# Key-innermost factors for the weight-table products of a two-layer PEER transformer kernel

## The chip, the cores and the metric

One core of one Trainium2 chip. The metric is the device time of one execution in microseconds. Three executions of the kernel before took 4184.06, 4193.06 and 4194.59 us; the median is 4193.06 us.

## The reference, cut to what matters

The reference is a transformer of two layers over 512 latent tokens and 256 context tokens, width 1024. Each layer is modulated by a conditioning vector (`silu(c) @ ada_w + ada_b`, six blocks of 1024 columns), has an attention (global in layer 0, windowed in layer 1), and ends in a PEER mixer: each token picks, in each of 8 heads, 16 of 128 x 128 experts, and mixes them with gates.

```python
def peer_block(hb, w_q, sub_keys, u_tab, v_tab):
    ...
    v1, i1 = lax.top_k(s1, PEER_TOPK)
    v2, i2 = lax.top_k(s2, PEER_TOPK)
    ...
    top_s, pos = lax.top_k(cand_s, PEER_TOPK)
    expert = jnp.take_along_axis(cand_i, pos, axis=-1)   # i1 * 128 + i2
    g = jax.nn.softmax(top_s, axis=-1)
    u = u_tab[expert]
    act = jax.nn.gelu(jnp.einsum('nhkd,nd->nhk', u, hb).astype(jnp.float32))
    w = (g * act).astype(hb.dtype)
    return jnp.einsum('nhk,nhkd->nd', w, v_tab[expert])
```

The output is the latent stream after both layers.

## The kernel before, in words

**Dense and sparse tokens.** Most tokens' PEER is computed densely, over all 16384 experts: a table G holds, for each token, the gate of each expert (zero where it isn't picked), and the dense part multiplies the gelu of `h @ u` by G before it multiplies by `v`. In layer 0 all 512 latent tokens (4 tiles of 128) are dense and the 256 context tokens are gathered one by one; in layer 1 the last 384 latent tokens (3 tiles) are dense and the first 128 are gathered.

**build_g** (L524) makes G for a tile of 128 tokens. Its input is a PSUM bank that `topk_resolve` (L478) leaves: for each of a token's 128 picks (8 heads x 16) the first key, the second key and the gate, with the pick on the partition axis. For a token, G is a product over the picks: one factor is the one-hot of the second key (128 picks x 128 keys), the other the one-hot of the first key times the gate, so 128 products of 128x128x128 for each tile. A step takes TB = 8 tokens: VectorE compares keys with a counter (`hot`, L547: both one-hots, bf16, laid out [pick, 2, key, token], token innermost), VectorE multiplies the first by the gate (`Eg`, L550, f32, [pick, key, token]), ScalarE casts the second to f32 (`B`, L552), and TensorE makes 8 products (`gm`, L557), four into a PSUM bank. A matmul reads its operands as `B[:, :, k]` and `Eg[:, :, k]`, so with a step of 8 floats from key to key. Each f32 product shows in the trace as two matmuls and two weight loads, 16 of each in a step. Banks are emptied one behind (LAG = 1) by ScalarE (L537): it reads the bank in its own order (token, then key) and writes `gsb` [key, 32 tokens] with the 32 tokens innermost, so 32 floats apart from key to key. After 4 steps (32 tokens) a `gsb` (2 buffers) is stored to the DRAM table Gd by SP's queue (L154, 2 MB).

**Buffers.** `hot` uses the tag "wh" and `B` the tag "wl", two buffers each, in the weight pool wp (layer 0) or gp (layer 1); `Eg` has two in gp. `topk_resolve` has one buffer each of the tags "hot" and "rep" in the pool kt: for each of its two key tables it writes `rep` (a copy by ScalarE, L511), `hot` (a comparison by VectorE, L513), multiplies them (L514) and sums on TensorE (L516).

**Conditioning.** `ada_load` (L180) issues 16 loads of 512 KB of `ada_w` on SP's queue, and `ada_cols` (L191) multiplies them with the conditioning vectors (`pr`, L198), transposes and adds the bias. Group 1 of layer 0 is loaded after the projections of its attention; groups 0 to 2 of layer 1 are loaded and multiplied after the build_g of the first three tiles of layer 0. All of these use the tag "wr" in the pool wp, WR = 4 buffers. `load_split` (L156) uses the same pool for projection weights: raw in "wr", its high and low halves in "wh" and "wl" (2 buffers each).

**Order of the work.** The kernel is written with a tile framework: each engine's instructions, and SP's queue of transfers, run in order, with semaphores set from the tiles that they touch. After build_g the dense part starts: it loads G back as `Gt` (L657), multiplies with `u` (`sp`) and `v` (`kp`, `op`), while gathers for the sparse tokens run on GpSimd. Some of its first weights (`Ur`, L154 to L162) are loaded and split during build_g.

Of the kernel before, what the change touches and what calls it, by code (L numbers as in the profile page):

```python
# [10 lines left out]
F32 = mybir.dt.float32  # L11
F32R = mybir.dt.float32r
BF16 = mybir.dt.bfloat16
U32 = mybir.dt.uint32
AF = mybir.ActivationFunctionType
ALU = mybir.AluOpType
# [4 lines left out]
P = 128  # L21
# [13 lines left out]
NK = 128  # L35
CB = 128
CBA = 512
# [5 lines left out]
TB = 8  # L43
# [16 lines left out]
WR = 4  # L60
# [9 lines left out]
def body(ctx, tc, xT_in, cT_in, ada_w, ada_b, gains1, gains2, w_qkv, qk_gain, w_o, sinks,  # L70
         w_pq, subk, u_t, u_n, v_b, v_n, ropeC, ropeS, ropeR, out):
    nc = tc.nc
    V, A, G, T = nc.vector, nc.scalar, nc.gpsimd, nc.tensor
# [7 lines left out]
    def bank(tag, name, bufs):  # L81
        return ps.tile([P, 512], F32, tag=tag, name=name, bufs=bufs)
# [9 lines left out]
    o = 0  # L92
# [10 lines left out]
    iota_t = const.tile([P, NK, TB], BF16, name="iota_t")  # L103
# [45 lines left out]
    def nm(s):  # L149
        uid[0] += 1  # L150
        return f"{s}_{uid[0]}"

    def dma(dst, src):
        nc.sync.dma_start(dst, src)  # L154
# [22 lines left out]
        modT = res.tile([P, 48, 2], F32, tag=f"mod{L}", name=nm("mod"))  # L177
        return modT

    def ada_load(L, grp, pool, bufs, between=None, tag="ar"):  # L180

        raws = []
        for i in range(16):
            if between:
                between(i)
            raw = pool.tile([P, 2, CBA], F32, tag=tag, name=nm(tag), bufs=bufs)
            dma(raw, ada_w[L, grp * 4 + i % 4, :, 2 * (i // 4):2 * (i // 4) + 2])
            raws.append(raw)
        return raws

    def ada_cols(L, modT, grp, pool, raws):  # L191


        pr = bank("S", nm("pr"), 2)
        for kt in range(DT):
            for j in range(4):
                js = slice(32 * j, 32 * j + 32)
                T.matmul(pr[js], cst[:, kt], raws[kt // 2 * 4 + j][:, kt % 2], start=kt == 0, stop=kt == DT - 1,  # L198
                         skip_group_check=True)
        rows = pool.tile([P, CBA], F32, tag="rows", name=nm("rows"), bufs=1)  # L200
        A.copy(rows, pr)
        pc = bank("bg", nm("pc"), 4)
        for i in range(4):
            T.transpose(pc[:, i * P:(i + 1) * P], rows[:, i * P:(i + 1) * P], ident)
        got = pc.rearrange("p (i j c) -> p j i c", j=4, c=32)[:, :, :, 0:2]
        blk = slice(grp * 16, grp * 16 + 16)
        bias = adb[:, L, blk].rearrange("p (j i) -> p j i", i=4)[:, :, :, None].to_broadcast([P, 4, 4, 2])
        V.tensor_tensor(modT[:, blk, :].rearrange("p (j i) c -> p j i c", i=4), got, bias, ALU.add)
# [312 lines left out]
    def flat(a):  # L521
        return a.rearrange("p h k -> p (h k)")

    def build_g(pt, Gd, t, gp, pe):  # L524


        ib = gp.tile([P, 2, P], BF16, tag="ib", name=nm("ib"), bufs=2)
        A.copy(ib.rearrange("p a b -> p (a b)"), pt[:, :2 * P])
        gt = gp.tile([P, P], F32, tag="gt", name=nm("gt"), bufs=2)
        A.copy(gt, pt[:, 2 * P:3 * P])  # L530
        full = [P, NK, TB]
        HT = TB // 2
        pending = []

        def evacuate():
            po, gs, o, b = pending.pop(0)
            A.copy(gs[:, :, o:o + HT].rearrange("p a t -> p t a"), po.rearrange("p (t a) -> p t a", t=HT))  # L537
            if o + HT == GB:
                dma(Gd[:, :, t * (P // GB) + b].rearrange("s p f -> p s f"),
                    gs.rearrange("p (s a) t -> p s (a t)", a=SC))  # L540

        for b in range(P // GB):
            gs = gp.tile([P, NK, GB], F32, tag="gsb", name=nm("gsb"), bufs=GSB)
            for n8 in range(GB // TB):
                tok = slice(b * GB + n8 * TB, b * GB + (n8 + 1) * TB)
                hot = pe.tile([P, 2] + full[1:], BF16, tag="wh", name=nm("hot"), bufs=2)
                V.tensor_tensor(hot, iota_t[:, None].to_broadcast([P, 2] + full[1:]),  # L547
                                ib[:, :, None, tok].to_broadcast([P, 2] + full[1:]), ALU.is_equal)
                Eg = gp.tile(full, F32, tag="Eg", name=nm("Eg"), bufs=2)
                V.tensor_tensor(Eg, hot[:, 0], gt[:, None, tok].to_broadcast(full), ALU.mult)  # L550
                B = pe.tile(full, F32, tag="wl", name=nm("B"), bufs=2)
                A.copy(B, hot[:, 1])  # L552
                for half in range(2):
                    po = bank("bg", nm("gm"), 4)
                    for i in range(HT):
                        k = half * HT + i
                        T.matmul(po[:, i * P:(i + 1) * P], B[:, :, k], Eg[:, :, k], start=True, stop=True)  # L557
                    pending.append((po, gs, (n8 * 2 + half) * HT, b))
                    if len(pending) > LAG:
                        evacuate()  # L560
        while pending:
            evacuate()
# [164 lines left out]
    mods = [ada_begin(L) for L in range(DEPTH)]  # L727
# [3 lines left out]
    for L in range(DEPTH):  # L731
        last = L == DEPTH - 1
        modT = mods[L]
        b1, g1, b2, g2 = (modT[:, i * DT:(i + 1) * DT, :] for i in (0, 2, 3, 5))
        stiles = list(range(SPARSE[L]))
        c0 = SPARSE[L] * P if last else 0
        nd = NLAT - c0
        groups = (LAT,) if last else (LAT, CTX)
        Gd = dram.tile([NK // SC, P, nd // GB, SC * GB], F32, tag=f"G{L}", name=nm("Gd"))
# [9 lines left out]
        if last:  # L749
            kt = kt_es.enter_context(pool(f"kt{L}"))  # L750
        wp = wp_es.enter_context(pool(f"wp{L}"))
        with pool(f"sp{L}") as sp, ExitStack() as a0_es:
            if L == 0:
                a0 = a0_es.enter_context(pool("a0"))
                def between(i):
                    if i in (4, 8):
                        half = slice(i - 4, i)
                        dma(xl[:, half], xT_in[:, half, :NLAT])
# [10 lines left out]
        with pool(f"ap{L}") as ap:  # L769
            r = qkv(L, wp, ap)  # L770
            if L == 0:
                ada_cols(0, modT, 1, wp, ada_load(0, 1, wp, WR, tag="wr"))
            if not last:
                attention(CTX, L, blocks_ctx, *r, ap, False)
                attention(LAT, L, blocks_global, *r, ap, False)
            else:
                attention(LAT, L, blocks_window, *r, ap, True)
# [16 lines left out]
        if not last:  # L794
            kt = kt_es.enter_context(pool(f"kt{L}"))
# [19 lines left out]
        with pool(f"gp{L}") as gp:  # L815
            for t in range(c0 // P, NLAT // P):
                topk_scan(tk["l", t], v12["l", t], 1, kt)
                pt = topk_resolve(tk["l", t], i12["l", t], kt, "bg", lambda i, shape: kt.tile(
                    shape, BF16, tag=("hot", "rep")[i], name=nm("hot"), bufs=1))
                build_g(pt, Gd, t - c0 // P, gp, gp if last else wp)  # L820
                if not last:
                    if t < 3:
                        ada_cols(1, mods[1], t, wp, ada_load(1, t, wp, WR, tag="wr"))
        if not last:
            kt_es.close()
            wp_es.close()
# [1 line left out]
        with pool(f"db{L}") as db:  # L828
            rb = rb_es.enter_context(pool(f"rb{L}", right=True))
            sg = groups[-1]["nm"]  # L830
            with pool(f"kc{L}") as kc:
                prep = []
                for t in stiles:
                    with later(SLACK2):
                        for hb in range(2):
                            topk_scan(tk[sg, t], v12[sg, t], hb, kc)
                        pt = topk_resolve(tk[sg, t], i12[sg, t], kc, "O", lambda i, shape: rb.tile(
                            shape, BF16, tag=("gu", "gv")[i], name=nm("hot"), bufs=(GUB, GVB)[i]))
# [90 lines left out]
```

## Time and profile before

| | us |
|---|---|
| median of 3 executions | 4193.06 |
| lowest, highest | 4184.06, 4194.59 |
| the profiled execution | 4188.21 |
| its span, first to last instruction | 4186.4 |
| TensorE matmul busy | 3962.7 (95%) |
| VectorE busy | 2979.7 (71%) |
| ScalarE busy | 1552.6 (37%) |
| GpSimd busy | 997.7 (24%) |
| mean granted clock of TensorE | 0.980 |

The profile names engines PE (TensorE matmuls), PEld (TensorE weight loads), DVE (VectorE), ACT (ScalarE), POOL (GpSimd) and SP (the transfers' queue). A group of instructions shows its line, engine, operation, output and inputs, shapes and count, then busy time and the mean of one in ns, then how long the engine sat idle before it and what ended that. A busy TensorE is not one at its peak: matmuls overlap, so the distance between two starts says more than the duration of one.

### The profile page before, as it was taken

The page shows a single profiled execution, that of the slowest core. Times are in us where ns is not written, and L with a number is a line of the kernel's source. Part 1 is how long each engine was busy: PE and PEld are TensorE (multiplying, and loading weights), DVE is VectorE, ACT ScalarE, POOL GpSimd, SP SyncE. Part 2 cuts the span into 40 slices and gives each one's busy share as a digit, 9 for nine tenths or more (in the row PEclk, how much of TensorE's full clock was granted, in tenths as well). Part 3 has the DMA queues.
Part 4 walks back from the last instruction along what each step waited for, and adds up shares of the span by engine and source line. Part 5 has one row for each costly group of instructions (what it writes and reads, how often), then busy time and mean ns, then how long its engine had stood idle before and what let it go on. Part 6 is the DMA issues. An engine that isn't in the chain of part 4 may idle for free.

```text
span 4186.4 us, 52018 instructions
## 1 busy us (share of the span) xinstructions
PE 3962.7 (95%) x19384; PEld 3405.7 (81%) x19384; DVE 2979.7 (71%) x5857; ACT 1552.6 (37%) x2271; POOL 997.7 (24%) x778
## 2 busy tenths in 40 slices
PE   7999898898899999999999989999998999999999
PEld 5667677687788777777777767768997999999999
DVE  3273796546688888888888754669657778787875
ACT  3162326556222222222222233534773333333332
POOL 0000000000344545444544300000002344443420
PEclk9999999999999999999999999999999999999999
DMA  4203125545699899989898831121457888888874
GB/s 175 97 20 112 56 79 167 166 136 175 209 323 329 315 316 322 327 315 316 316 330 310 285 107 60 32 74 36 131 144 260 286 292 299 302 300 297 299 270 157
DMA packets 343406, 894.08 MB, mean 214 GB/s; under 512 B 25968, under 2 KB 145904, under 8 KB 338800
## 3 DMA queue, kind: packets, MB, share of 16 engines
q1 hardware_dynamic: 232560, 488.05, 34.2%
q0 software_dynamic: 110592, 402.70, 28.1%
q8 instruction: 152, 2.49, 0.2%
q14 instruction: 102, 0.84, 0.1%
HBM read 826.16 MB, written 64.49 MB: 213 GB/s over the span
## 4 chain that ended last, share of the span: by engine, by line
PE 57%; issue 16%; DMA 11%; POOL 7%; DVE 7%; ACT 2%; SPq 0%; POOLq 0%; DVEq 0%; ACTq 0%
PE gm L557 10%; DMA gv<-v_n,idx 6%; PE sp L168 5%; PE sp L170 5%; PE sp L169 5%; PE pj L168 4%; PE pj L169 4%; PE pj L170 4%; POOL gu L593 4%; POOL gv L593 3%; DMA gu<-u_n,idx 3%; PE kp L676 2%; PE kp L678 2%; PE kp L677 2%; PE op L678 2%
## 5 line engine op out<-in xcount | busy, mean ns | idle before, releaser
L593 POOL DMA_INDIRECT gu<-u_n,idx x384 | 544.6, 1418 | 2816.2 <-DVE idx L573 1070.1
L168 PE MATMUL sp<-hil,Uh 128*128 128x512 f32 (+1 forms) x2048 | 751.5, 367 | 27.1 <-ACT act L654 27.1
L169 PE MATMUL sp<-lol,Uh 128*128 128x512 f32 (+1 forms) x2048 | 752.0, 367 | 0.0
L170 PE MATMUL sp<-hil,Ul 128*128 128x512 f32 (+1 forms) x2048 | 746.7, 365 | 4.2 <-DVE Ul L162 4.2
L621 DVE SCALAR_TENSOR_TENSOR acc<-gv,w,acc 128x1024 f32<-128x1024 f32 x381 | 490.0, 1286 | 134.7 <-DMA gv<-v_n,idx 133.9
L662 ACT CAST wh<-act 128x512 fp32r<-128x512 f32 (+1 forms) x256 | 145.0, 567 | 1034.2 <-DVE act L660 1026.2
L593 POOL DMA_INDIRECT gv<-v_n,idx x384 | 450.0, 1172 | 327.6 <-DVE acc L621 220.6
L611 DVE CUSTOM_DVE_ANT_0 gu<-gu,hn 128x1024 f32<-128x1024 f32 x384 | 468.5, 1220 | 69.1 <-DMA gu<-u_n,idx 68.4
L557 PEld LDWEIGHTS gm<-Eg,B 128*128 128x128 f32 x1792 | 432.4, 337 | 25.9 <-issue 11.4
L557 PE MATMUL gm<-Eg,B 128*128 128x128 f32 x1792 | 439.7, 422 | 11.1 <-DVE Eg L550 10.8
L168 PEld LDWEIGHTS sp<-hil,Uh 128*128 128x128 f32 x2048 | 387.3, 189 | 75.7 <-ACT act L654 28.1
L162 DVE TENSOR_TENSOR Ul<-Ur,Uh 128x1024 fp32r<-128x1024 f32 x256 | 312.5, 1221 | 190.7 <-ACT Uh L160 190.6
L170 PEld LDWEIGHTS sp<-hil,Ul 128*128 128x128 f32 x2048 | 387.2, 189 | 50.8 <-DVE Ul L162 6.1
L677 PE MATMUL kp<-wh,Vl 128*128 128x512 f32 (+1 forms) x1024 | 378.5, 370 | 49.8 <-DVE Vl L162 49.8
L169 PEld LDWEIGHTS sp<-lol,Uh 128*128 128x128 f32 x2048 | 387.8, 189 | 40.6 <-issue 2.5
L160 ACT CAST Uh<-Ur 128x1024 fp32r<-128x1024 f32 x256 | 268.9, 1051 | 395.3 <-PE sp L169 389.7
L676 PE MATMUL kp<-wh,Vh 128*128 128x512 f32 (+1 forms) x1024 | 376.3, 368 | 1.7 <-ACT wh L662 1.3
L678 PE MATMUL kp<-wl,Vh 128*128 128x512 f32 (+1 forms) x1024 | 376.1, 367 | 0.0
L676 PE MATMUL op<-wh,Vh 128*128 128x512 f32 (+1 forms) x1024 | 371.4, 363 | 0.3 <-DVE xl L647 0.3
L677 PE MATMUL op<-wh,Vl 128*128 128x512 f32 (+1 forms) x1024 | 370.5, 362 | 0.0
L678 PE MATMUL op<-wl,Vh 128*128 128x512 f32 (+1 forms) x1024 | 370.5, 362 | 0.0
L160 ACT CAST Vh<-Vr 128x1024 fp32r<-128x1024 f32 x256 | 268.8, 1050 | 222.5 <-PE op L678 186.1
(223 smaller groups left out, 6554.9 us busy)
## 6 DMA issues: line engine op xcount, KB each, us to landing
Ur<-u_t SPq DMA_DIRECT2D x256, 512.0 KB, 5.9
Vr<-v_b SPq DMA_DIRECT2D x256, 512.0 KB, 6.6
Gd<-gsb SPq DMA_DIRECT2D x28, 2048.0 KB, 9.3
wr<-ada_w SPq DMA_DIRECT2D x64, 512.0 KB, 5.4
Gt<-Gd SPq DMA_DIRECT2D x32, 1024.0 KB, 8.1
Gt<-Gd SPq DMA_DIRECT2D x32, 768.0 KB, 7.1
ar<-ada_w SPq DMA_DIRECT2D x32, 512.0 KB, 10.2
wr<-w_pq SPq DMA_DIRECT2D x32, 512.0 KB, 3.6
```

The costliest lines, as they stand in the source:

```text
L160: A.copy(hi, raw)
L162: V.tensor_tensor(lo, raw, hi, ALU.subtract)
L168: T.matmul(o, sh, mh, start=i == 0, stop=False)
L169: T.matmul(o, sh, ml, start=False, stop=False)
L170: T.matmul(o, sl, mh, start=False, stop=i == n - 1)
L557: T.matmul(po[:, i * P:(i + 1) * P], B[:, :, k], Eg[:, :, k], start=True, stop=True)
L593: G.indirect_dma_start(out=r, out_offset=None, in_=tab, in_offset=bass.IndirectOffsetOnAxis(ap=idx[:, s:s + 1], axis=0))
L611: V.tensor_tensor_reduce(out=r, in0=r, in1=hn, scale=1.0, scalar=0.0, op0=ALU.mult, op1=ALU.add, accum_out=sd[:, k:k + 1])
L621: V.scalar_tensor_tensor(acc[ti], r, w[:, k:k + 1], acc[ti], ALU.mult, ALU.add)
L676: T.matmul(o[:, :n], vh[:, k, ds], wh, start=start, stop=False, skip_group_check=True)
L677: T.matmul(o[:, :n], vl[:, k, ds], wh, start=False, stop=False, skip_group_check=True)
L678: T.matmul(o[:, :n], vh[:, k, ds], wl, start=False, stop=stop, skip_group_check=True)
```

## The change

The one-hots keep their layout, token innermost, but the two f32 factors are written as [pick, token, key], so that a matmul reads `second[:, k]` and `first[:, k]` as 128 contiguous floats. The product with the gate (VectorE) and the cast (ScalarE) therefore read `hot` with a step of 8 bf16 from key to key. The bank is read with the token innermost (512 bytes apart) and `gsb` is written in groups of four contiguous floats; each fourth bank is emptied by VectorE. The one-hots of the steps alternate between the tags "hot" and "rep" of the pool kt, one buffer each, which topk_resolve uses too. "wh" and "wl" of wp are no longer used by build_g, and the conditioning loads that took 4 buffers of "wr" take 8 in turn: 4 of "wr", 2 of "wh", 2 of "wl".

```diff
-    def ada_load(L, grp, pool, bufs, between=None, tag="ar"):
+    def ada_load(L, grp, pool, bufs, between=None):
...
-            raw = pool.tile([P, 2, CBA], F32, tag=tag, name=nm(tag), bufs=bufs)
+            tag, n = ("ar", bufs) if bufs else (("wr", WR), ("wr", WR), ("wh", 2), ("wl", 2))[i // 2 % 4]
+            raw = pool.tile([P, 2, CBA], F32, tag=tag, name=nm(tag), bufs=n)
...
-    def build_g(pt, Gd, t, gp, pe):
+    def build_g(pt, Gd, t, gp, kp):
...
-            A.copy(gs[:, :, o:o + HT].rearrange("p a t -> p t a"), po.rearrange("p (t a) -> p t a", t=HT))
+            count[0] += 1
+            eng = V.tensor_copy if count[0] % 4 == 0 else A.copy
+            eng(gs[:, :, o:o + HT], po.rearrange("p (t a) -> p a t", t=HT))
...
-                hot = pe.tile([P, 2] + full[1:], BF16, tag="wh", name=nm("hot"), bufs=2)
-                V.tensor_tensor(hot, iota_t[:, None].to_broadcast([P, 2] + full[1:]),
-                                ib[:, :, None, tok].to_broadcast([P, 2] + full[1:]), ALU.is_equal)
-                Eg = gp.tile(full, F32, tag="Eg", name=nm("Eg"), bufs=2)
-                V.tensor_tensor(Eg, hot[:, 0], gt[:, None, tok].to_broadcast(full), ALU.mult)
-                B = pe.tile(full, F32, tag="wl", name=nm("B"), bufs=2)
-                A.copy(B, hot[:, 1])
+                hot = kp.tile([P, 2, NK, TB], BF16, tag=("hot", "rep")[n8 % 2], name=nm("hot"), bufs=1)
+                V.tensor_tensor(hot, iota_t[:, None].to_broadcast([P, 2, NK, TB]),
+                                ib[:, :, None, tok].to_broadcast([P, 2, NK, TB]), ALU.is_equal)
+                first = gp.tile([P, TB, NK], F32, tag="first", name=nm("first"), bufs=2)
+                V.tensor_tensor(first, hot[:, 0].rearrange("p a t -> p t a"),
+                                gt[:, tok, None].to_broadcast([P, TB, NK]), ALU.mult)
+                second = gp.tile([P, TB, NK], F32, tag="second", name=nm("second"), bufs=2)
+                A.copy(second, hot[:, 1].rearrange("p a t -> p t a"))
...
-                        T.matmul(po[:, i * P:(i + 1) * P], B[:, :, k], Eg[:, :, k], start=True, stop=True)
+                        T.matmul(po[:, i * P:(i + 1) * P], second[:, k], first[:, k], start=True, stop=True)
...
-                ada_cols(0, modT, 1, wp, ada_load(0, 1, wp, WR, tag="wr"))
+                ada_cols(0, modT, 1, wp, ada_load(0, 1, wp, 0))
...
-                build_g(pt, Gd, t - c0 // P, gp, gp if last else wp)
+                build_g(pt, Gd, t - c0 // P, gp, kt)
...
-                        ada_cols(1, mods[1], t, wp, ada_load(1, t, wp, WR, tag="wr"))
+                        ada_cols(1, mods[1], t, wp, ada_load(1, t, wp, 0))
```

## Rows read from the trace of the kernel before

**Rows 1.** The page, chain that ended last: shares by engine, then by line.
```profile
PE 57%; issue 16%; DMA 11%; POOL 7%; DVE 7%; ACT 2%; SPq 0%; POOLq 0%; DVEq 0%; ACTq 0%
PE gm L557 10%; DMA gv<-v_n,idx 6%; PE sp L168 5%; PE sp L170 5%; PE sp L169 5%; PE pj L168 4%; PE pj L169 4%; PE pj L170 4%; POOL gu L593 4%; POOL gv L593 3%; DMA gu<-u_n,idx 3%; PE kp L676 2%; PE kp L678 2%; PE kp L677 2%; PE op L678 2%
```

**Rows 2.** Line 557: its durations (min/median/max), its waits, and who waited (us, times).
```profile
L557 PEld LDWEIGHTS gm<-Eg,B x1792: 312/338/343, 643.7 to 3130.5; 128*128 128x128 f32 x200
...
  DVE Eg L550: 10.8, 4
...
who waited for it (us, times):
  DVE Eg L550: 180.3, 98
  ACT gsb L537: 143.8, 149
```

**Rows 3.** Stretches, all engines: us; PE, PEld, DVE, ACT, POOL busy; clock; DMA; GB/s.
```profile
640.00:990.00 350.00, 319.42 (x1376) 276.78 (x1375) 185.72 (x257) 209.75 (x225) 0.00 (x0) 0.97 0.51 153
...
794.00:826.00 32.00, 19.62 (x92) 8.43 (x92) 15.77 (x52) 9.48 (x13) 0.00 (x0) 0.84 0.69 222
...
2908.00:3132.00 224.00, 217.89 (x985) 216.41 (x985) 138.81 (x172) 163.94 (x179) 0.00 (x0) 0.98 0.43 122
```

**Rows 4.** The same stretches, line 557 alone: us; PE, PEld busy; clock; DMA; GB/s.
```profile
640.00:990.00 350.00, 252.68 (x1024) 247.32 (x1024) 0.97 0.51 153
2908.00:3132.00 224.00, 187.05 (x768) 185.08 (x768) 0.98 0.43 122
```

**Rows 5.** Timeline in build_g: start, us, engine, line, operation, shapes, count.
```profile
670.59 15.43 PEld L557 LDWEIGHTS gm<-Eg,B 128*128 128x128 f32 x64 [0.84 <-issue]
```

**Rows 6.** Timeline in peer_q: products of the same shape, operands contiguous.
```profile
593.04 0.97 PEld L439 LDWEIGHTS s<-skb,pq 128*128 128x128 f32 x8 [0.23 <-ACT pq L436]
```

**Rows 7.** Groups by line and form, ScalarE.
```profile
L537 ACT COPY gsb<-gm 128x512 f32<-128x512 f32 x224 | 232.0, 1036 | 145.7 <-PE gm L557 143.8
L552 ACT CAST B<-hot 128x1024 f32<-128x1024 bf16 x112 | 118.8, 1062 | 7.1 <-DVE hot L547 7.0
...
L405 ACT COPY pT<-pt 128x512 f32<-128x512 f32 x48 | 27.5, 588 | 18.2 <-PE pt L398 18.2
```

**Rows 8.** Groups by line and form, VectorE.
```profile
L550 DVE TENSOR_TENSOR Eg<-hot,gt 128x1024 f32<-128x1024 bf16 x112 | 136.6, 1225 | 180.3 <-PE gm L557 180.3
L547 DVE TENSOR_TENSOR hot<-iota_t,ib 128x2048 bf16<-128x2048 bf16 x112 | 132.0, 1219 | 3.6 <-ACT ib L528 3.4 <-ACT B L552 0.2
...
L405 DVE COPY pT<-pt 128x256 f32<-128x256 f32 x32 | 13.4, 419 | 3.3 <-PE pt L398 2.7
...
L387 DVE TENSOR_TENSOR su<-su 128x1 f32<-128x1 f32 x48 | 7.6, 158 | 12.6 <-ACT pr L383 12.6
...
L405 DVE COPY pT<-pt 128x128 f32<-128x128 f32 x16 | 4.6, 290 | 3.0 <-PE pt L398 3.0
...
L485 DVE COPY gs<-ts 128x8 f32<-128x8 f32 x10 | 1.6, 160 | 0.0
```

**Rows 9.** Timeline in build_g, VectorE: two comparisons in a row.
```profile
670.86 2.35 DVE L547 TENSOR_TENSOR hot<-iota_t,ib 128x2048 bf16<-128x2048 bf16 x2
```

**Rows 10.** Timeline at the first tile border: a copy and a comparison of topk_resolve.
```profile
719.31 1.90 ACT L511 COPY hot<-dif 128x2048 bf16<-128x2048 bf16 x1
...
785.34 1.22 DVE L513 TENSOR_TENSOR hot<-posb,first_pos 128x2048 bf16<-128x2048 bf16 x1
```

**Rows 11.** Waits from 590 to 1000 us: us in total, times, longest.
```profile
PE pr L198 <- DMA wr<-ada_w: 19.4, 8, 11.1
```

**Rows 12.** Waits from 160 to 210 us: us in total, times, longest.
```profile
PE pr L198 <- DMA wr<-ada_w: 8.5, 6, 3.1
```

**Rows 13.** The page, DMA issues: count, KB each, median us to landing.
```profile
Gd<-gsb SPq DMA_DIRECT2D x28, 2048.0 KB, 9.3
wr<-ada_w SPq DMA_DIRECT2D x64, 512.0 KB, 5.4
```

More of the change, by code (lines that the diff above doesn't have):

```diff
@@ L530, in build_g @@
         A.copy(gt, pt[:, 2 * P:3 * P])
-        full = [P, NK, TB]
         HT = TB // 2
         pending = []
+        count = [0]
         def evacuate():
             po, gs, o, b = pending.pop(0)
-            A.copy(gs[:, :, o:o + HT].rearrange("p a t -> p t a"), po.rearrange("p (t a) -> p t a", t=HT))
+            count[0] += 1
+            eng = V.tensor_copy if count[0] % 4 == 0 else A.copy
+            eng(gs[:, :, o:o + HT], po.rearrange("p (t a) -> p a t", t=HT))
             if o + HT == GB:
```

## The prediction

> **What bounds the kernel now.** The clock comes first: TensorE's granted clock is 0.97 and 0.98 in the two stretches that matter [rows 3], its upper level (2.4 GHz), so it is not the issue. The chain that ended last comes second: TensorE has 57% of it, and its largest single line is L557, the small products of build_g, with 10% [rows 1]; 10% of the 4186 us span is some 420 us. Third, who waits for whom at L557: VectorE's Eg (L550) waited 180 us for these matmuls and ScalarE's gsb copy (L537) 144 us, while the matmuls themselves sat idle 11 us for Eg and nearly nothing else [rows 2]. So in build_g TensorE sets the pace. Fourth, how long that is: build_g runs in 640 to 990 us (layer 0, 4 tiles, 64 steps of 8 tokens) and 2908 to 3132 us (layer 1, 3 tiles, 48 steps); L557 alone is busy 252.7 and 187.1 us there [rows 4].
>
> Fifth, why it is slow. Undisturbed, 64 weight loads (4 steps) take 15.43 us [rows 5], so 0.24 us for each and 3.84 us for the 16 of a step. The products of peer_q have the same shape and type (128x128x128 f32), but operands that lie contiguous: 8 weight loads take 0.97 us [rows 6]. With a load's own 0.19 us taken off the end, 7 spacings take 0.78 us: 0.111 us each. In build_g each operand B[:, :, k] and Eg[:, :, k] is read with 8 floats, 32 bytes, from one key to the next. That is the only difference that I find between the two.
>
> **The change, part by part.** *Matmuls.* The same 1792 instructions, with the operands contiguous. At 0.111 us a step takes 16 x 0.111 = 1.78 us of TensorE instead of 3.84. TensorE then no longer sets the pace, and the question is which of the other two engines does.
>
> *VectorE, per step.* The comparison (hot, L547) stays: two in a row take 2.35 us, one of them 1.22, so the second adds 1.13 [rows 8, 9]. The product with the gate, `first` (Eg before, L550, 1.225 us), has as many elements and still writes contiguously, but reads the bf16 hot 16 bytes apart. Its lower bound is 1.13 us, as now; the upper one comes from the weight load: (0.240 - 0.111)/128 = 1.01 ns more per strided element, times 1024 is 1.03 us more, so 2.16 us. I take 1.13: the row is the same instruction with as many elements, and a copy of 8 elements 64 bytes apart takes 160 ns against 158 for an operation on one [rows 8]. These rows are small and of different operations, so both ends are kept. One bank in four now goes to VectorE, half a bank per step. A copy of 256 elements from a bank takes 419 ns and of 128 takes 290: 1.01 ns per element, so 0.68 us for 512. For the stride I add what ScalarE now pays for its own: 1.036 us for the strided bank copy against 0.588 for a plain 128x512 one, 0.45 us more [rows 7, 8]. That gives 1.13 us, bounds 0.68 and 1.58 (twice the excess); half is 0.56. Sum: 1.13 + 1.13 + 0.56 = 2.82 us, bounds 2.60 and 4.08.
>
> *ScalarE, per step.* The cast `second` (B, 1.06 us) also reads 16 bytes apart: 1.06 to 2.09. One and a half bank copies remain: now they write four floats together but read the bank 512 bytes apart. I keep 1.04, the same copy with its stride on the other side; bounds 0.59 and 1.48. Sum: 1.06 + 1.5 x 1.04 = 2.62, bounds 1.95 and 4.31.
>
> So VectorE sets 2.82 us per step: (3.84 - 2.82) x 112 = **114 us less**. The 144 us of both stretches that are no steps (574 - 112 x 3.84) stay in length: TensorE's other work inside them (66.7 and 30.8 us [rows 3, 4]) now hides under VectorE, while VectorE's own other work (the scan of the next tile, the Ul splits) comes into the open. VectorE's other work is 56 us there (324.5 busy [rows 3], less 112 times the two instructions of rows 8). I put the two against each other, with 20 us either way.
>
> What the rule would make of `first`: the Trainium skill (SBUF — State Buffer, section Door 1: The DMA port swizzle) says that SBUF lines are 16 bytes, and that a stream which goes to a new line at each access pays for it. Here every read of hot by key does that, so the rule speaks for the upper end; the weight loads agree with it at 32 bytes, and no row shows it for VectorE's reads at 16. By the row that I take the sum is 4070 us, by the rule it is rival 1's, below.
>
> *hot in two single buffers shared with topk_resolve.* The steps alternate between "hot" and "rep", so as many are in flight as before. But now a tile's resolve can't start its rep copy (1.90 us, L511) before the last steps have let go of that buffer. Before, ScalarE made it a whole tile early, at 719 us, while the comparison that needs it came at 785 [rows 10]. It now stands beside that comparison (1.22 us) at each of 5 tile borders: about 2 us each, **10 us more**, bounds 0 and 20.
>
> *Conditioning loads in 8 buffers.* TensorE waits 19.4 us for them in layer 0's stage, and 8.5 us of its 28 us at 178 to 206, where attention stands behind them on TensorE [rows 11, 12]. Half of that goes, **14 us less**, bounds 0 and 28: buffers wh and wl come free only when the last projections have been multiplied. On SP's queue the loads stand in line with the Gd stores, so an earlier load also frees a store behind it. The stores themselves have as many bytes; each lands in 9.3 us [rows 13], under four new steps (11.3 us), so two gsb buffers still cover it, with only 2 us to spare.
>
> The profiled execution took 4188.2 us, 5 below the median of the runs shown. Sum: 4188 - 114 + 10 - 14 = **4070 us**. What comes after each stretch (the dense part) starts as much earlier, since its first matmuls wait for Gt, read from Gd.
>
> **The rivals.**
> 1. *VectorE reads slowly by key.* With `first` at 2.16 us the step takes 1.13 + 2.16 + 0.56 = 3.85 us, and the whole gain of the steps is gone: 4185 us; half the excess gives 4127. For it: TensorE's weight loads. Against: the two small copies above. The rule cited above gives this same outcome.
> 2. *ScalarE becomes the bound, and slower than TensorE was.* The place is its queue of cast and bank copies. It decides from the point where cast + 1.5 bank copies pass 3.84 us: with the cast at 2.09 that is a bank copy over 1.17 us. At 1.48, twice the excess, the step takes 4.31 us: 112 x 0.47 = 53 more, so 4237 us. For it: ScalarE's excess on strided writes [rows 7], and that it is now asked for two kinds of strided reads. Against: bank copies lose their strided writes, and a quarter of them.
>    The Trainium skill (PSUM — Partial Sum Buffer, section Specifications (TRN2)) gives PSUM lines of 8 bytes and says that non-contiguous patterns slow matmuls a lot; whether a copy out of a bank pays too, no row shows.
> 3. *Transfers become the bound in layer 0.* A tile writes 8 MB of G and loads 8 MB of weights for the next layer. If a store takes 16 us beside the loads instead of 11.3 for its four steps, 12 stores x 4.7 = 56 us come back: 4126 us. For it: the queues move 222 GB/s at a tile's border [rows 3]. Against: the DMA engines are 51% busy over that stretch.
> 4. *The change doesn't quicken the loads,* because the stride is not what slows them; all stays at some 4185 us. Against it: rows 6.
>
> **How the numbers follow.** The forecast has 0.47 and its own range of 4030 to 4105 (the bank copy at its lower bound takes 25 off, the small terms move the rest), rival 1 0.22, rival 2 0.13, rival 3 0.12, rival 4 0.06. I predict 4070 us. The range leaves out rival 2 and the lowest edge of the forecast: 4035 to 4195. 0.3%, some 12.6 us, is about what a measurement can tell from no change. Faster by more: the forecast, rival 3 and half of rival 1, 0.70. Within: the other half and most of rival 4, 0.16. Slower: rival 2 and a rest, 0.14.
>
> **What would show it right or wrong.** Weight loads of the small products 0.11 us apart, no longer followed by VectorE waiting for TensorE; `first` near 1.2 us and a bank copy near 1.0; VectorE without gaps through a tile, and 16 steps in some 45 us instead of 61. Wrong: `first` over 2 us (rival 1), bank copies over 1.2 with VectorE waiting on ScalarE's order (rival 2), gsb copies waiting for Gd stores (rival 3), weight loads still at 0.24 us (rival 4).

## The result, and the profile after

The changed kernel takes 4044.27 us (median of 4 runs, 4038.29 to 4048.38) against 4192.49 us before (a fourth run added to the three above): a ratio of 0.9649, 95% interval 0.9629 to 0.9669. So it is 148 us faster; 4070 us had been forecast. The profiled execution took 4048.38 us with a span of 4046.6, so 139.8 us less span than before.

The chain that ended last, on the page of the changed kernel (shares by engine, then by line):

```profile
PE 49%; issue 19%; DVE 13%; DMA 10%; POOL 8%; ACT 2%; POOLq 0%; SPq 0%; DVEq 0%; ACTq 0%
PE sp L170 5%; DMA gv<-v_n,idx 5%; PE sp L168 5%; PE sp L169 5%; DVE first L554 4%; POOL gv L598 4%; POOL gu L598 4%; PE pj L168 4%; PE pj L169 4%; PE pj L170 4%; DMA gu<-u_n,idx 3%; PE kp L682 2%; PE kp L683 2%; PE kp L681 2%; PE op L683 2%
```

The small products (now line 562) led this list with 10% [rows 1] and are gone from it; VectorE's `first` has come in with 4%, and VectorE's share rose from 7 to 13%. The waits of line 562 in the changed kernel (durations as min/median/max, then us and times) show the same reversal:

```profile
L562 PEld LDWEIGHTS gm<-first,second x1792: 186/192/338, 629.9 to 2993.2; 128*128 128x128 f32 x200
L562 PE MATMUL gm<-first,second x1792: 270/275/553, 629.9 to 2993.3; 128*128 128x128 f32 x200
...
  DVE first L554: 88.1, 78
  ACT second L557: 82.7, 44
...
  ACT gsb L541: 42.0, 46
...
who waited for it (us, times):
  ACT gsb L541: 41.7, 54
```

Before, VectorE waited 180 us for these products and they waited 11 us for it [rows 2]. Now they wait 88 us for VectorE, 83 us for the cast and 42 us for ScalarE's bank copies. Of the waits for them, ScalarE's 42 us for a bank are left (last line), and none of VectorE's for `first`. Undisturbed, 16 weight loads now take 1.86 us (timeline, TensorE's weight loads):

```profile
2991.49 1.86 PEld L562 LDWEIGHTS gm<-first,second 128*128 128x128 f32 x16 [0.67 <-ACT gsb L541]
```

Less a load's own 0.19 us, that is 0.111 us for each of 15 spacings, exactly the row of the contiguous products [rows 6]. The stretches of build_g (us; PE, PEld, DVE, ACT, POOL busy; clock; DMA; GB/s):

```profile
626.00:882.00 256.00, 195.69 (x1358) 160.63 (x1355) 250.28 (x294) 205.38 (x198) 0.00 (x0) 0.92 0.65 197
2790.00:2995.00 205.00, 145.25 (x1064) 134.76 (x1063) 201.83 (x274) 164.93 (x164) 0.00 (x0) 0.95 0.48 135
```

VectorE is busy for 98% of both, where TensorE was for 91 and 97% [rows 3]. What it is busy with stands in the groups by line and form from 626 to 884 us (busy us, mean ns, idle time before):

```profile
L557 ACT CAST second<-hot 128x1024 f32<-128x1024 bf16 x64 | 130.0, 2067 | 8.5 <-DVE hot L551 8.5
L554 DVE TENSOR_TENSOR first<-hot,gt 128x1024 f32<-128x1024 bf16 x64 | 129.0, 2022 | 0.0
L551 DVE TENSOR_TENSOR hot<-iota_t,ib 128x2048 bf16<-128x2048 bf16 x64 | 75.7, 1233 | 0.6 <-ACT ib L530 0.6
L541 ACT COPY gsb<-gm 128x512 f32<-128x512 f32 x96 | 55.3, 590 | 24.0 <-PE gm L562 23.2
L541 DVE COPY gsb<-gm 128x512 f32<-128x512 f32 x32 | 22.2, 695 | 1.0 <-PE gm L562 1.0
```

`first` rose from 1225 to 2022 ns and the cast from 1062 to 2067 [rows 7, 8]: reading `hot` 16 bytes apart makes the one 65% and the other 95% longer. The bank copies went the other way, ScalarE's from 1036 [rows 7] to 590. The pace is read from VectorE's timeline in a tile (start, us, line, count):

```profile
638.89 2.34 DVE L551 TENSOR_TENSOR hot<-iota_t,ib 128x2048 bf16<-128x2048 bf16 x2
641.16 2.07 DVE L554 TENSOR_TENSOR first<-hot,gt 128x1024 f32<-128x1024 bf16 x1
643.14 0.69 DVE L541 COPY gsb<-gm 128x512 f32<-128x512 f32 x1
643.74 2.04 DVE L554 TENSOR_TENSOR first<-hot,gt 128x1024 f32<-128x1024 bf16 x1
645.66 2.38 DVE L551 TENSOR_TENSOR hot<-iota_t,ib 128x2048 bf16<-128x2048 bf16 x2
```

There is no gap, and two steps take 645.66 - 638.89 = 6.77 us: 3.38 us a step, against TensorE's 3.84 before and the 2.82 forecast.

**Where the time went.** The timeline of the small products' weight loads gives three parts for each stage: its length from the first to the last, the gaps at tile borders (over 10 us each), and the rest, which belongs to the steps. Layer 0 went from 344.1 to 250.3 us: borders 73.0 to 46.4, steps 271.1 to 203.9. Layer 1 went from 218.9 to 185.7: borders 26.2 to 33.4, steps 192.7 to 152.3. Together the steps give 107.6 us, the borders 19.4; the first product of layer 0 starts 13.9 us earlier. That sums to 140.9 us; what lies between and behind the two stages became 1.1 us longer, which makes the span's 139.8. Per step this is 4.14 us before (463.8/112) and 3.18 now (356.2/112).

Neither figure is the bare pace of its engine. Before, 0.30 us a step came on top of 3.84: between the steps TensorE also did products of the conditioning columns and of the next stage, and idled 0.84 us [rows 5] as it returned from them. Now that work lies beside VectorE's. And a tile's first step is prepared while the border lasts, so 16 steps span 15 paces and one set of products: 15 x 3.38 + 1.9 = 52.6 us, 51.0 measured (203.9/4).

### The profile page after: what moved, and what is told of

Its sections match the earlier page's. It is cut to its first block, busy times and chain, and to the rows that moved or that the text cites. A ratio compares the mean times of both kernels' runs of the same rounds, so it can differ in the third digit from the quotient of the medians.

```text
span 4046.6 us, 52056 instructions
## 1 busy us (share of the span) xinstructions
PE 3753.2 (93%) x19384; PEld 3200.5 (79%) x19384; DVE 3091.0 (76%) x5913; ACT 1536.2 (38%) x2217; POOL 1000.8 (25%) x778
## 4 chain that ended last, share of the span: by engine, by line
PE 49%; issue 19%; DVE 13%; DMA 10%; POOL 8%; ACT 2%; POOLq 0%; SPq 0%; DVEq 0%; ACTq 0%
PE sp L170 5%; DMA gv<-v_n,idx 5%; PE sp L168 5%; PE sp L169 5%; DVE first L554 4%; POOL gv L598 4%; POOL gu L598 4%; PE pj L168 4%; PE pj L169 4%; PE pj L170 4%; DMA gu<-u_n,idx 3%; PE kp L682 2%; PE kp L683 2%; PE kp L681 2%; PE op L683 2%
## 5 line engine op out<-in xcount | busy, mean ns | idle before, releaser
L562 PE MATMUL gm<-first,second 128*128 128x128 f32 x1792 | 239.9, 292 | 98.0 <-DVE first L554 88.1
L562 PEld LDWEIGHTS gm<-first,second 128*128 128x128 f32 x1792 | 223.9, 204 | 126.8 <-ACT second L557 79.3
```

What stands on the lines that cost most here:

```text
L562: T.matmul(po[:, i * P:(i + 1) * P], second[:, k], first[:, k], start=True, stop=True)
```

## The experiments

All ratios are to the kernel before, run beside each. Line numbers are those of the changed kernel where the edit leaves them; times of steps and borders are read from the weight loads as above.

**1. The loads back in 4 buffers.**

```diff
-            tag, n = ("ar", bufs) if bufs else (("wr", WR), ("wr", WR), ("wh", 2), ("wl", 2))[i // 2 % 4]
+            tag, n = ("ar", bufs) if bufs else ("wr", WR)
```

> The changed kernel with its conditioning loads back in 4 buffers (tag wr alone); everything else stays. The changed kernel took 4044 us. Theory: the extra buffers are worth more than the 13 us by which the first attention came earlier, because layer 0's stage of build_g became 94 us shorter and its 64 steps explain only some 30 of that (0.47 us each); TensorE's wait for the loads at the tile borders fell from 19 to 4 us. Then this kernel takes 4075 to 4100 us, and the wait for wr at TensorE is back at 15 us or more in layer 0's stage. Rival: the borders got shorter because TensorE's work there is now hidden under VectorE's; then only the first attention is later, by 13 us: 4057 us, and layer 0's stage stays at 251 us.

Measured: 4057.54 us, ratio 0.9688 (0.9667 to 0.9709), 13 us over the changed kernel (16 by the ratios). Attention's first product, by its group in the changed kernel (first and last start at the end of the line):

```profile
L368 PEld LDWEIGHTS sc<-kTl,qTl x224: 186/190/333, 213.1 to 2592.9; 128*128 128x128 f32 x112
```

and in this one:

```profile
L368 PEld LDWEIGHTS sc<-kTl,qTl x224: 186/190/338, 225.4 to 2600.7; 128*128 128x128 f32 x112
```

TensorE's wait for a load in "wr" from 150 to 215 us (us in total, times, longest), first in the changed kernel, then in this one:

```profile
PE pr L200 <- DMA wr<-ada_w: 1.5, 1, 1.5
...
PE pr L200 <- DMA wr<-ada_w: 8.6, 5, 3.2
```

Attention starts 12.3 us later, and the wait is back at its length of before [rows 12]; in the changed kernel the loads in "wh" and "wl" add only 0.7 us to the 1.5. Layer 0's stage stays at 249.3 us, with 45.6 us of borders. The theory falls and the rival holds: in this kernel the buffers are worth the 13 us ahead of attention and nothing in build_g.

**2. All banks on ScalarE.**

```diff
-            eng = V.tensor_copy if count[0] % 4 == 0 else A.copy
+            eng = A.copy
```

> The changed kernel with every bank copied out by ScalarE. Theory: VectorE alone sets the pace at 3.37 us a step, of which half a bank copy is 0.35. It then needs 3.03, and ScalarE 2.03 + 2 x 0.58 = 3.19, which becomes the bound: 0.18 us x 112 steps = 20 us less, 4024 us. Rival: VectorE and ScalarE hold each other up in order (cast behind two copies, copies behind matmuls), so that the copy on VectorE was the better place: no change or slower, 4044 to 4065 us, with first or hot waiting for ScalarE.

Measured: 4014.19 us, ratio 0.9588 (0.9565 to 0.9612): 30 us less than the changed kernel (26 by the ratios). VectorE's timeline:

```profile
655.87 2.37 DVE L551 TENSOR_TENSOR hot<-iota_t,ib 128x2048 bf16<-128x2048 bf16 x2
658.13 3.96 DVE L554 TENSOR_TENSOR first<-hot,gt 128x1024 f32<-128x1024 bf16 x2
662.01 2.35 DVE L551 TENSOR_TENSOR hot<-iota_t,ib 128x2048 bf16<-128x2048 bf16 x2
```

Two steps take 662.01 - 655.87 = 6.14 us, 0.31 us less a step. The theory holds in that VectorE's pace is what counts, and the fourth of the banks that the change gave it costs the change some 30 us. Its second half falls: ScalarE didn't become the bound. Its casts and copies fit in beside each other, with little to spare: from 655 to 680 us VectorE is busy for all 25.0 us and ScalarE for 23.5.

**3 and 4. One stride each.** Experiment 3 writes and reads only `first` (the moving operand) with the token innermost, experiment 4 only `second` (the stationary one, the weights). The shape of the tile and the instruction that writes it follow.

```diff
-                        T.matmul(po[:, i * P:(i + 1) * P], second[:, k], first[:, k], start=True, stop=True)
+                        T.matmul(po[:, i * P:(i + 1) * P], second[:, k], first[:, :, k], start=True, stop=True)
```

```diff
-                        T.matmul(po[:, i * P:(i + 1) * P], second[:, k], first[:, k], start=True, stop=True)
+                        T.matmul(po[:, i * P:(i + 1) * P], second[:, :, k], first[:, k], start=True, stop=True)
```

> The changed kernel, but the moving operand first is written and read with the token innermost, as before; only the stationary operand second has its key innermost. Theory: the weight load is what the stride of 32 bytes slows, the moving operand's stride costs TensorE nothing. Then a step's 16 weight loads are 0.11 to 0.13 us apart, first takes 1.22 instead of 2.02 us, VectorE needs 2.57 us a step and ScalarE 2.03 + 1.5 x 0.58 = 2.90, which sets the pace: 0.47 us x 112 = 53 us less, 3992 us. Rival: the moving operand's stride slows the products as well; then TensorE is back at 3.8 us a step and the time at some 4095 us.

> The counterpart: only the moving operand first has its key innermost; the stationary operand second has the token innermost, as before. Theory (the stationary stride is the cost): weight loads are again 0.24 us apart, TensorE sets 3.84 us a step, 0.47 more than now: 53 us more, 4097 us, and first waits for the products. Rival (the moving stride is the cost): products at 0.11 to 0.13 us, VectorE still sets 3.37 us a step, 4044 us, with second back at 1.06 us.

Measured: 4160.69 us (ratio 0.9936, 0.9916 to 0.9957) for experiment 3 and 4142.07 us (0.9892, 0.9871 to 0.9913) for experiment 4. Experiment 3's durations (ns, min/median/max):

```profile
L562 PEld LDWEIGHTS gm<-first,second x1792: 186/208/338, 631.1 to 3097.0; 128*128 128x128 f32 x200
L562 PE MATMUL gm<-first,second x1792: 390/412/582, 631.1 to 3097.3; 128*128 128x128 f32 x200
```

and a row of the timeline of its weight loads:

```profile
658.67 7.28 PEld L562 LDWEIGHTS gm<-first,second 128*128 128x128 f32 x32 [0.84 <-issue]
```

The durations of experiment 4:

```profile
L562 PEld LDWEIGHTS gm<-first,second x1792: 312/335/338, 630.5 to 3088.9; 128*128 128x128 f32 x200
L562 PE MATMUL gm<-first,second x1792: 272/402/599, 630.6 to 3089.0; 128*128 128x128 f32 x200
```

and a row of its timeline:

```profile
658.66 15.31 PEld L562 LDWEIGHTS gm<-first,second 128*128 128x128 f32 x64 [0.84 <-ACT second L557]
```

With the moving operand strided the load itself is quick (208 ns) and the product slow (412 against 275 after the change), and the spacing is (7.28 - 0.21)/31 = 0.228 us. With the weights strided the load is slow (335 ns), and the spacing is (15.31 - 0.34)/63 = 0.238 us. Both strided gave 0.24. So in experiment 3 the theory falls and the rival holds, and in experiment 4 the theory holds for the pace: either stride alone brings back nearly all of the cost. Over 0.111 us the excess is 0.117 with one stride, 0.127 with the other and 0.129 with both, so the two don't add up: loads and products lie beside each other. Steps take 4.27 and 4.19 us in layer 0, against 4.24 before (271.1/64): what these kernels still gain is not in the steps. Both are some 45 to 65 us over the figures expected, which had counted a step at 3.84 and left out what TensorE does between steps: over both layers the steps take 116 and 100 us more than in the changed kernel, where some 50 had been expected.

**5 and 6. The rest of the change alone.** Both factors with the token innermost, banks copied by ScalarE in the old order; `hot` stays in the buffers shared with topk_resolve, and `second` in buffers of its own in gp, not in "wl". Experiment 5 has the 8 load buffers, 6 has 4.

```diff
-                        T.matmul(po[:, i * P:(i + 1) * P], second[:, k], first[:, k], start=True, stop=True)
+                        T.matmul(po[:, i * P:(i + 1) * P], second[:, :, k], first[:, :, k], start=True, stop=True)
...
-            eng = V.tensor_copy if count[0] % 4 == 0 else A.copy
-            eng(gs[:, :, o:o + HT], po.rearrange("p (t a) -> p a t", t=HT))
+            eng = A.copy
+            eng(gs[:, :, o:o + HT].rearrange("p a t -> p t a"), po.rearrange("p (t a) -> p t a", t=HT))
```

> The changed kernel with both factors written with the token innermost and the banks copied by ScalarE as before; what is left of the change is hot in the two buffers shared with topk_resolve and the conditioning loads in 8 buffers. Theory: TensorE sets 3.84 us a step again and the loads are worth the 13 us ahead of the first attention and, where TensorE has no slack, up to the 27 us by which layer 0's tile borders (73 us in the kernel before) exceed those of the changed kernel (46): 4150 to 4165 us. Rival: the borders were shortened by the faster products alone; then this kernel only gains the 13 us, 4177 us, and its borders take 70 us or more.

> The same with the conditioning loads in 4 buffers: of the change only the place of hot is left. Theory: sharing hot's buffers with topk_resolve costs at most 2 us at each of 5 tile borders, 10 us in all: 4190 to 4200 us, and the borders of layer 0 are back at 73 us. Rival: the borders were long because of where hot and B lay; then the borders stay short here too, and the time is at some 4165 us.

Measured: 4147.21 us, ratio 0.991 (0.9886 to 0.9933), and 4170.87 us, ratio 0.9963 (0.995 to 0.9976). Layer 0's borders take 41.6 us in experiment 5 and 59.4 in 6. So with the old products the 8 buffers are worth 24 us, not 13, as the theory for 5 had it (its range was 3 us too slow). For 6 the theory falls: what is left of the change doesn't cost 10 us, it came with 15 us less. The time is near the rival's 4165, its borders halfway between. TensorE's wait for the loads in layer 0's stage of experiment 6:

```profile
PE pr L200 <- DMA wr<-ada_w: 4.1, 2, 2.9
```

The longest such wait before was 11.1 us [rows 11]; it stood in the middle border, which took 33.4 us and takes 12.6 here, while the first border became longer (11.7 to 17.3). Layer 0's borders together are 13.6 us shorter, nearly all of the 15 us; that one longest wait is 8 us shorter. Why the load comes earlier here stays open, and also whether the place of `hot` or that of `second` brings it; neither was tried alone with the old products.

**7. The bank order alone undone,** on the kernel of experiment 2.

```diff
-            eng(gs[:, :, o:o + HT], po.rearrange("p (t a) -> p a t", t=HT))
+            eng(gs[:, :, o:o + HT].rearrange("p a t -> p t a"), po.rearrange("p (t a) -> p t a", t=HT))
```

> The kernel with every bank on ScalarE (4014 us), its banks read as they lie and written with gaps, as before the change. Theory: the gaps make a bank copy 1.04 us instead of 0.58, ScalarE needs 2.03 + 2 x 1.04 = 4.1 us a step where some 3.1 set the pace: 1.0 x 112 = 112 us more, some 4125 us, and first and second wait for nothing but ScalarE. Rival: the bank order is hidden behind VectorE: 4014 to 4030 us.

Measured: 4092.0 us, ratio 0.9773 (0.9753 to 0.9793): 78 us over experiment 2. ScalarE's timeline:

```profile
657.91 2.23 ACT L557 CAST second<-hot 128x1024 f32<-128x1024 bf16 x1
659.89 2.15 ACT L541 COPY gsb<-gm 128x512 f32<-128x512 f32 x2
661.67 2.17 ACT L557 CAST second<-hot 128x1024 f32<-128x1024 bf16 x1
663.59 2.14 ACT L541 COPY gsb<-gm 128x512 f32<-128x512 f32 x2
665.35 2.25 ACT L557 CAST second<-hot 128x1024 f32<-128x1024 bf16 x1
```

ScalarE has no gap and sets (665.35 - 657.91)/2 = 3.72 us a step; 0.65 over experiment 2's 3.07, times 112, is 73 us. The theory holds, with a smaller size, since a cast and the copies behind it overlap: each begins 0.25 to 0.38 us before the one ahead has ended, which the sum of their durations left out.

**8. Token by token.** Cast and `hot` go; 16 instructions on VectorE write both factors in place.

```diff
...
+                    V.tensor_scalar(first[:, i], iota_k, ib[:, 0, j:j + 1], gt[:, j:j + 1], ALU.is_equal, ALU.mult)
...
+                    V.tensor_scalar(second[:, i], iota_k, ib[:, 1, j:j + 1], None, ALU.is_equal)
...
```

> No strided read at all: VectorE writes first and second with the key innermost token by token, one comparison of 128 keys with one token's key for each (first multiplies by the gate in the same instruction); hot and the cast on ScalarE go, ScalarE copies all banks. 16 small instructions replace 3.1 us of VectorE a step. Theory: a small one takes 0.16 us (the shortest rows of VectorE), 2.5 us a step, VectorE still sets the pace: 0.6 us x 112 = 67 us less than the kernel with every bank on ScalarE, some 3947 us. Rival: each pays its start, 0.29 us as the copies of 128x128 do; 4.6 us a step, 170 us more, some 4180 us.

Measured: 4075.31 us, ratio 0.9738 (0.9712 to 0.9764), 61 us over experiment 2. VectorE's timeline:

```profile
662.04 1.65 DVE L559 TENSOR_SCALAR second<-iota_k,ib 128x128 f32<-128x128 bf16 x8
663.60 2.13 DVE L555 TENSOR_SCALAR first<-iota_k,ib,gt 128x128 f32<-128x128 bf16 x8
665.65 1.65 DVE L559 TENSOR_SCALAR second<-iota_k,ib 128x128 f32<-128x128 bf16 x8
```

In a row one that writes a token of `second` takes (663.60 - 662.04)/8 = 0.195 us and one that writes `first`, with the gate, (665.65 - 663.60)/8 = 0.256, between the two expectations: 3.61 us a step. The theory falls; small instructions are no way out here.

**9 and 10. Compare with the key innermost.** From experiment 2: `hot` itself is written as [token, key], so neither factor reads with a stride. `iota_k` holds the keys 0 to 127 in a row. In experiment 9 each token's key lies twice side by side in `ib`; in 10 it lies once and is repeated by a stride of 0.

```diff
...
+        ib = gp.tile([P, 2, P, 2], BF16, tag="ib", name=nm("ib"), bufs=2)
+        A.copy(ib.rearrange("p a b c -> p (a b) c"), pt[:, :2 * P, None].to_broadcast([P, 2 * P, 2]))
...
+                    V.tensor_tensor(hot[:, s].rearrange("p t (a c) -> p t a c", c=2),
+                                    iota_k.rearrange("p (a c) -> p a c", c=2)[:, None].to_broadcast([P, TB, NK // 2, 2]),
+                                    ib[:, s, tok, None].to_broadcast([P, TB, NK // 2, 2]), ALU.is_equal)
...
```

```diff
...
+                    V.tensor_tensor(hot[:, s], iota_k[:, None].to_broadcast([P, TB, NK]),
+                                    ib[:, s, tok, None].to_broadcast([P, TB, NK]), ALU.is_equal)
...
```

> From the kernel with every bank on ScalarE (4014 us, two steps in 6.13 us): hot itself is compared with the key innermost, so that neither first nor second reads with a stride. Each token's key lies twice side by side, so that the comparison reads two neighbours of it for each two neighbouring keys; it is two instructions of 1024 elements. Theory: the strided reads are what VectorE and ScalarE pay; first is back at 1.22 us, second at 1.06, the comparisons keep their pace (1.13 us for 2048): VectorE 2.4 us a step, ScalarE 1.06 + 2 x 0.58 = 2.2. 0.65 us x 112 = 73 us less: 3941 us. Rival: the comparison loses its pace when it no longer runs along 8 neighbours, 1.1 us for each 1024, so 2.2 + 1.15 = 3.35 us a step: some 4045 us.

> The same with the token's key once, repeated along the 128 keys by the access pattern (stride 0), without the pairs. Theory: a comparison that doesn't read two neighbours from each input takes 1.04 to 1.2 us for 1024 elements, as first does: 2.2 + 1.15 = 3.35 us a step, some 4045 us, first and second as in the kernel with pairs. Rival: a repeated element costs nothing, and the time is that of the kernel with pairs.

Measured: 3948.61 us, ratio 0.943 (0.9406 to 0.9455), with the pairs; 4073.74 us, 0.9735 (0.9709 to 0.9761), without. Experiment 9's groups (ns, min/median/max):

```profile
L558 DVE TENSOR_TENSOR first<-hot,gt x112: 1211/1216/1227, 623.5 to 2889.7; 128x1024 f32<-128x1024 bf16 x112
L560 ACT CAST second<-hot x112: 1040/1048/1105, 623.6 to 2890.6; 128x1024 f32<-128x1024 bf16 x112
L554 DVE TENSOR_TENSOR hot<-iota_k,ib x224: 674/682/693, 622.3 to 2889.1; 128x1024 bf16<-128x1024 bf16 x112
L543 ACT COPY gsb<-gm x224: 578/587/654, 626.1 to 2893.8; 128x512 f32<-128x512 f32 x112
```

and VectorE's timeline in it:

```profile
657.95 1.22 DVE L558 TENSOR_TENSOR first<-hot,gt 128x1024 f32<-128x1024 bf16 x1
659.08 1.28 DVE L554 TENSOR_TENSOR hot<-iota_k,ib 128x1024 bf16<-128x1024 bf16 x2
660.28 1.22 DVE L558 TENSOR_TENSOR first<-hot,gt 128x1024 f32<-128x1024 bf16 x1
```

The comparisons of experiment 10:

```profile
L554 DVE TENSOR_TENSOR hot<-iota_k,ib x224: 1208/1216/1227, 624.7 to 3014.2; 128x1024 bf16<-128x1024 bf16 x112
```

and VectorE's timeline there:

```profile
665.43 2.35 DVE L554 TENSOR_TENSOR hot<-iota_k,ib 128x1024 bf16<-128x1024 bf16 x2
667.70 1.22 DVE L557 TENSOR_TENSOR first<-hot,gt 128x1024 f32<-128x1024 bf16 x1
668.84 2.35 DVE L554 TENSOR_TENSOR hot<-iota_k,ib 128x1024 bf16<-128x1024 bf16 x2
```

With contiguous reads `first` and the cast are back at 1.22 and 1.05 us, and a step takes 660.28 - 657.95 = 2.33 us on VectorE. This version is 96 us faster than the changed kernel and 238 us faster than the one before; the theory holds. Without the pairs two comparisons take 2.35 instead of 1.28 us, and a step 668.84 - 665.43 = 3.41. The theory for 10 holds on the comparison; the time is 29 us over its figure, and 0.34 us more a step explains only 38 of the 60 us over experiment 2. The timeline of the weight loads shows where the rest lies:

```profile
871.55 1.86 PEld L564 LDWEIGHTS gm<-first,second 128*128 128x128 f32 x16 [1.81 <-ACT second L559]
875.22 1.86 PEld L564 LDWEIGHTS gm<-first,second 128*128 128x128 f32 x16 [1.81 <-ACT second L559]
```

The sets of products start mostly 3.67 us apart, not 3.41, and each waits for its cast. The cast stands on ScalarE behind two bank copies, which wait for the products of the step before, so here that ring of ScalarE and TensorE is slower than VectorE. Over both layers the steps take 65 us more than in experiment 2, the borders 4 less.

**11. `hot` in buffers of its own,** on the kernel of experiment 1.

```diff
-                hot = kp.tile([P, 2, NK, TB], BF16, tag=("hot", "rep")[n8 % 2], name=nm("hot"), bufs=1)
+                hot = kp.tile([P, 2, NK, TB], BF16, tag="wh", name=nm("hot"), bufs=2)
...
-                build_g(pt, Gd, t - c0 // P, gp, kt)
+                build_g(pt, Gd, t - c0 // P, gp, gp if last else wp)
```

> The changed kernel with its conditioning loads in 4 buffers (0.9688 of the kernel before) and hot back in two buffers of its own (tag wh, which those loads leave free). It prices the sharing with topk_resolve alone. Theory, the prediction's term: sharing costs about 2 us at each of 5 tile borders, so this kernel is up to 10 us faster, 4047 to 4057 us, 0.966 to 0.969. Rival: sharing gains, as it seemed to with the old products (4171 against 4186 us, and borders of 59 against 73 us), since topk_resolve comes later and stands less in front of the steps: 4065 to 4075 us, 0.971 to 0.974, with borders of layer 0 longer than 46 us.

Measured: 4059.72 us, ratio 0.9697 (0.9684 to 0.9711) against experiment 1's 0.9688 (0.9667 to 0.9709), layer 0's borders 45.0 against 45.6 us. No difference can be told from the times, whose intervals leave room for a gain of some 7 us and a loss of some 14; the borders of both layers, 76.5 against 79.0 us, give 2.5. So neither the theory's 10 us nor the rival's longer borders are there: with quick products the sharing costs next to nothing.

## Why the prediction was right

The sign and the time were right, and so was the core of the mechanism: TensorE set the pace through the strided operands, they now load at 0.111 us, and VectorE is the new bound. But the size was right in part by luck, by terms that erred in opposite directions. Of the forecast's 118 us, VectorE's slower pace took away 63 (0.56 x 112); TensorE's other work in the steps brought 56 more, the borders 19 and the sharing that cost nothing 10: that makes the 140 us of the span. By the prediction's own signs rival 1 came in part: `first` takes over 2 us, and 16 steps take 51 us, not 45.

*Matmuls* held to the third digit, and rival 4 is out. Naming the stride as the only difference was right; experiments 3 and 4 add that both operands' strides had to go.

*VectorE, per step* was wrong: 2.82 us forecast, 3.38 measured. The step that failed is "I take 1.13" for `first`, drawn from copies of 8 elements. It measured 2.02, near the upper end of 2.16 that came from the weight load and that rival 1 carried. So rival 1's price was the right one. Its time of 4185 us was wrong mainly because 3.84 was not what a step cost before; besides, the half bank copy is 0.35 us, not 0.56 (0.695 for one, at the lower bound of 0.68), and `first` 2.02, not 2.16.

*ScalarE, per step:* the cast met its upper bound (2.07 against 2.09) and the bank copy its lower (0.59). A strided read of SBUF cost about what a strided write had, 0.98 against 0.88 ns more per element, and a read of the bank 512 bytes apart cost nothing. Experiment 7 shows that the second was needed: without it, and with all banks on ScalarE, ScalarE becomes the bound, as rival 2 has it, though at 3.72 us a step, under the 3.84 that rival 2 asks for.

*The stages' other work* was set to even, with 20 us either way. That term carried the sum: by bare paces, (3.84 - 3.38) x 112 = 52 us, the change would have gained 65 with the loads. Instead the steps gave 107.6 us, mainly since TensorE's products in between (0.30 us a step) and each tile's first step now lie beside other work, and the borders gave another 19.4. Experiment 1 shows that the loads had no part in this. The reason the prediction gave for the even sum, VectorE's 56 us in the open, counted work that mostly lies in the borders: in the changed kernel 49 of the 64 us that VectorE is busy in the two stages with other lines than 541, 551 and 554.

*hot in shared buffers:* 10 us forecast, no difference in time and 2.5 us in the borders measured (experiment 11). *Loads in 8 buffers:* 14 us forecast, 13 measured (experiment 1); the place was the one named, ahead of attention, while the other half of the term's bound, in layer 0's stage, counts only with slow products (experiment 5). Rival 3 is out: `first` has no idle time ahead of it in layer 0's stretch, and no bank copy waited for a store, so no store holds the pace.

On the rule that the prediction weighed: the Trainium skill (SBUF — State Buffer, section Door 1: The DMA port swizzle) says that a stream pays at each new line of 16 bytes. The runs agree for both engines and for TensorE's operands: 1.225 to 2.022, 1.062 to 2.067, and 0.111 to 0.228 or 0.238 us. The bank copies fit too: ScalarE writes groups of four floats, 16 bytes, at 128 bytes from group to group as quickly as contiguous ones (0.590 against 0.588 us), while single floats at that distance took 1.036. No run has groups of another length, so how long a line is stays open here. The rule deserved the higher chance.

## What to carry to other kernels

When a transposed layout helps one engine, the transposition has to be paid somewhere. Price the strided side at the nearest strided row of the trace, even one of another engine, rather than at the contiguous row of the same instruction; then look for the producer that can write the wanted order at full pace, as the doubled key did here. And if the bound moves from one engine to another, the first engine's odd jobs between the steps fall away with it: take the pace before from first to last instruction of a tile, not from an undisturbed run of them. A load buffer's worth, too, is a property of what it waits beside: 24 us with slow products, 13 with quick ones.

## What the runs showed of the hardware

- A matmul pays for the stride of either operand, at 32 bytes from element to element: the load takes 335 instead of 192 ns, or the product 412 instead of 275 ns, and they follow each other at 0.238 or 0.228 us instead of 0.111. The two don't add up (0.240 with both), so mending one alone gains next to nothing: 4161 and 4142 us (experiments 3 and 4) against 4147 with neither mended (experiment 5).
- Reading a bank 512 bytes apart is free for both engines (128x512 in 0.590 us on ScalarE, where a plain copy took 0.588 [rows 7], and in 0.695 on VectorE, where the plain ones of half and a quarter of the size lead to 0.68 [rows 8]), with SBUF written in groups of four floats; writing single floats 128 bytes apart cost 1.036.
- A comparison of bf16 takes 0.682 us for 1024 elements when its reads come in neighbouring pairs, and 1.216 when one input is repeated by a stride of 0. The Trainium skill (VectorE: DVE Perf Modes, section What auto-detection actually checks) says that the engine does two elements at a time if every tensor is 16-bit with a step of plus or minus 1; the runs agree. They also show that an innermost run of two is enough.
- The granted clock in build_g's stretches fell from 0.97 and 0.98 of the upper level, 2.4 GHz, [rows 3] to 0.92 and 0.95, with TensorE busy for 76 and 71% of them instead of 91 and 97. What that costs in all was not measured; VectorE, which sets the pace there, has no gap in the timeline above. At a border it can be seen: TensorE was busy for 3.9 of the 8 us from 750 to 758; from 758.5 to 761.2 us the granted clock was 0.50, the lower level of 1.2 GHz, and the products of lines 168 to 170 started 0.42 to 0.43 us apart; from 761.7 to 763.5 it was 1.00, and they started 0.23 to 0.24 us apart.
